# Streaming encoder trunk on one core: the last output's transposes one tile later, later splits and sums in the FFNs, one PSUM pool for two FFNs, first weights by halves of k

## The chip, the cores and the metric

The kernel runs on one core of one Trainium2 chip. The core has five engines with a queue of instructions each: PE (matrix products and transposes), DVE (VectorE), ACT (ScalarE), POOL (GpSimd) and SP (SyncE), whose queue here issues the DMAs. The metric is the device time of one execution in microseconds (us), lower is better. All names with an L and a number are lines of the kernel's file before the change; lines of the changed file are said to be so.

## The reference

One inference step of a hybrid encoder of two layers, for 512 new frames of one stream (with no history) and 16 frames each of 8 running streams, 640 tokens in all, with D_MODEL = 1024 and D_FF = 2816, all in float32:

```python
def swiglu(x, w_gate, w_up, w_down):
    return (jax.nn.silu(x @ w_gate) * (x @ w_up)) @ w_down
...
    for l in range(DEPTH):
        x = x + 0.5 * swiglu(rmsnorm(x, norm_g[l, 0]), ffn_w_gate[l, 0], ffn_w_up[l, 0], ffn_w_down[l, 0])
        hn = rmsnorm(x, norm_g[l, 1])
        if l % 2 == 0:
            out, ab_state = mixer_ab(hn, ab_state, ab_w_in, ab_w_out, ...)
        else:
            out, c_state = mixer_c(hn, c_state, gdn_w_in, gdn_w_out, ...)
        x = x + out
        x = x + 0.5 * swiglu(rmsnorm(x, norm_g[l, 2]), ffn_w_gate[l, 1], ffn_w_up[l, 1], ffn_w_down[l, 1])
    return rmsnorm(x, norm_f), ab_state, c_state
```

mixer_ab is an mLSTM beside a Mamba-2 SSD, mixer_c a gated DeltaNet. The change touches neither of them: it touches the four FFNs (the SwiGLU blocks), the start, and the last output with the last RMSNorm.

## The kernel before, in words

**Tiles.** x lives in SBUF for the whole run, transposed: eight tiles x[0] to x[7] of 128 features by 640 tokens. Two halves of 320 tokens (HT) go through PE as two matmuls, each into a PSUM bank of its own (`small`, 8 banks in an FFN).

**Products in float32.** PE takes every fp32 operand as a high and a low part (type fp32r) and makes three passes, high by high, high by low, low by high. A weight of 128x512 is *split*: ACT copies the high part (L614; L207 in the mixers and the last output), POOL subtracts it from the source for the low part (L615, L208). The parts go to a pool `wsp` of eight tiles, that is four splits. For the activations, x times the norm's gain, ACT makes the high part and DVE the low part; the factor 1/rms is multiplied in after the product.

**Stages.** Six, one after the other: FFN, mLSTM with SSD, FFN, FFN, gated DeltaNet, FFN. Each opens its own pool of PSUM banks (eight in an FFN, another layout in a mixer), so the first banks of a stage wait for the last use of those before.

**An FFN.** `first_jobs` works the first pair of column tiles (256 columns of gate and up) by plain products: four jobs `loop(0)` to `loop(3)` run over two tiles of x each, for the gate (four banks) and the first half of up (two banks), then `second(0)` and `second(1)` for the other half of up (two banks). Each split of these covers 128x512 of a weight. After `loop(3)` PE makes the sums of squares into the factors 1/rms, which DVE finishes (`rstd_cols`, from L363). Beside the loops, `loop_end(m)` makes for one pair of x tiles the block sums T that the other pairs of columns need: ACT scales both tiles (L329), DVE makes four sums (L331 to L334), ACT and DVE make high and low parts of three (L319, L320). After `loop(3)`, `loop_end` also copies the four gate banks to SBUF on ACT (L526). The silu of the first pair (L551) and its hidden product come in pieces later (`rest`).

The ten other pairs of columns go by seven products of half blocks each (a Strassen-like scheme). DVE makes the sums of weights S for it (L408, L409, L412, L415); PE makes seven block products of 12 matmul pairs (L425); DVE combines the banks. A pair ends with `hidden`: DVE multiplies gate and up (L481), ACT makes the high part of h (L483), DVE the low part (L486). Between two pairs, a job of `down_jobs` for each of four tiles of x multiplies the h of the *group before* by the down weights (L492, into two banks) and DVE adds half of each bank to x (L577). Groups are of one pair first, then two pairs.

**What sets the order.** `pipe` writes the jobs out in order: for each job its matmuls (`run`), then the sums of weights that are soon due, then its `post` (what follows on ACT and DVE), then as many splits as the freed `wsp` tiles allow, and last the load of the next weights into the raw tile whose last split this was. The instructions of each engine are chained in that order:

```python
                job.run()
                to = ready(n)
                sums(to + SUMS)
                if job.post is not None:
                    job.post()
                split(to)
            if job.then is not None:
                job.then()
```

An instruction that waits so holds everything behind it on its engine. What stands outside `pipe` (the mixers, the start, the last output) is ordered by a scheduler.

**The start.** `load_x` issues the loads on SP's queue: x in four chunks of 256 features (`xg4` to `xg7`), the gains, and the first 256 columns of gate and up in halves of 128 columns (all of k, 1024). PE transposes x (L283), DVE or ACT copies it from PSUM (L286), ACT makes the high parts of x times the gain (L307), DVE the low parts (L308), then squares and their sum for the norm (L296, L299, L300).

**The last output.** `finish` takes the last group of down products (four tiles of h) and the last RMSNorm, for three token tiles (384 columns) and then for two (256). For each of the eight tiles of x: 12 matmuls into a bank (L2081), DVE adds it to x (L2083), ACT squares x (L2088; L2086 for the first tile) and scales it by the gain (L2091), DVE adds the square to the sum (L2089), PE transposes the scaled tile (L2095), and DVE and ACT copy the rows out by turns (L2098). `output` makes the factors from the sum, multiplies the rows and stores them.

## Time and profile before

| | us |
|---|---|
| median of three runs | 3036.93 |
| lowest and highest | 3025.48, 3037.0 |
| the profiled execution's own time | 3035.38 |
| its span (first to last instruction) | 3033.7 |
| PE busy in the span | 2901.8 |
| DVE busy | 1884.2 |
| POOL busy | 1474.1 |
| ACT busy | 1255.1 |

The mean clock granted to PE is 0.977 of full speed. In the rows that the prediction quotes, a list of waits gives the instruction that waits, the one waited for, and then the sum in us, how often, and the longest. A row of windows gives the window, its length, the busy time and count of PE, PE's weight loads, DVE, ACT and POOL, the granted clock, the busy share of the DMA engines and GB/s. A row of the timeline gives the start, the length, the engine and the line, and in brackets how long the engine had waited and for what. Names ahead of an arrow are what is written, behind it what is read.

### The profile page before, as it was taken

How to read it: one execution, taken by the hardware profiler on the slowest of the kernel's cores; microseconds unless marked ns; L12 is line 12 of the kernel's file. 1: busy time of each engine (PE TensorE's matmuls, PEld its weight loads, DVE VectorE, ACT ScalarE, POOL GpSimd, SP SyncE). 2: the span in 40 equal slices, each digit the busy share in tenths (PEclk: the TensorE clock that was granted, in tenths of full speed). 3: DMA queues.
4: the chain of work that ended last, by engine and by line, in shares of the span. 5: the costliest groups of instructions: out<-in, count | busy, mean ns of one | idle time of the engine just before them, and what ended most of it. 6: DMA issues, size and time to landing. Idle time of an engine off the chain costs nothing. (4 is left out here: it accounts for less than half of the span.)

```text
span 3033.7 us, 51436 instructions
## 1 busy us (share of the span) xinstructions
PE 2901.8 (96%) x19910; PEld 2784.1 (92%) x19910; DVE 1884.2 (62%) x3547; ACT 1255.1 (41%) x2655; POOL 1474.1 (49%) x1039
## 2 busy tenths in 40 slices
PE   7999999999999999999998999999999999999995
PEld 7999998988989889999998999999888898899994
DVE  7666655233566677666656666657777656766654
ACT  5333334333344344333344333335555455333334
POOL 3766662322223126677635766734222223676672
PEclk9999999999999999999999999999999999999999
DMA  3222222222223222222222222221221312222222
GB/s 102 88 76 82 84 84 58 86 86 86 83 59 89 69 80 67 92 78 82 84 72 63 94 84 79 75 67 49 63 67 46 87 51 88 77 84 76 79 64 82
DMA packets 245160, 232.14 MB, mean 77 GB/s; under 512 B 22135, under 2 KB 221956, under 8 KB 244918
## 3 DMA queue, kind: packets, MB, share of 16 engines
q1 hardware_dynamic: 244918, 228.87, 24.6%
q8 instruction: 158, 2.59, 0.4%
q14 instruction: 84, 0.69, 0.1%
HBM read 210.23 MB, written 18.60 MB: 75 GB/s over the span
## 5 line engine op out<-in xcount | busy, mean ns | idle before, releaser
L615 POOL TENSOR_TENSOR wsp<-wraw,wsp 128x512 fp32r<-128x512 f32 x600 | 887.0, 1489 | 608.2 <-ACT wsp L614 561.3
L208 POOL TENSOR_TENSOR wsp<-wraw,wsp 128x512 fp32r<-128x512 f32 x216 | 291.4, 1357 | 848.1 <-ACT wsp L207 511.1
L425 PE MATMUL small<-xg,wsp 128*128 128x320 f32 x3840 | 593.3, 312 | 20.3 <-ACT wsp L614 8.5
L492 PE MATMUL small<-h,wsp 128*128 128x320 f32 x4032 | 597.9, 309 | 0.0
L425 PEld LDWEIGHTS small<-xg,wsp 128*128 128x128 f32 x3840 | 575.0, 190 | 24.2 <-ACT wsp L614 19.5
L492 PEld LDWEIGHTS small<-h,wsp 128*128 128x128 f32 x4032 | 593.1, 188 | 0.0
L614 ACT ACTIVATE wsp<-wraw 128x512 fp32r<-128x512 f32 x600 | 364.4, 626 | 361.5 <-PE small L425 218.5
L225 PE MATMUL big<-xg,wsp 128*128 128x320 f32 x2112 | 370.2, 323 | 0.0
L225 PEld LDWEIGHTS big<-xg,wsp 128*128 128x128 f32 x2112 | 323.2, 194 | 21.8 <-issue 20.7
L615 POOL TENSOR_TENSOR wsp<-S,wsp 128x512 fp32r<-128x512 f32 x160 | 253.6, 1597 | 47.0 <-ACT wsp L614 36.0
L425 PE MATMUL small<-extA,wsp 128*128 128x320 f32 x1440 | 253.9, 312 | 1.0 <-POOL wsp L615 0.9
L767 PE MATMUL big<-wsp,xg 128*128 128x256 f32 x1920 | 244.1, 284 | 1.5 <-DVE zs L2061 1.4
L452 DVE TENSOR_TENSOR up<-small,up 128x320 f32<-128x320 f32 x200 | 97.7, 488 | 225.9 <-PE small L425 225.9
L767 PEld LDWEIGHTS big<-wsp,xg 128*128 128x128 f32 x1920 | 233.0, 188 | 4.2 <-DVE zs L2061 2.1
L207 ACT ACTIVATE wsp<-wraw 128x512 fp32r<-128x512 f32 x216 | 136.2, 633 | 227.9 <-PE big L225 101.7
L425 PEld LDWEIGHTS small<-extA,wsp 128*128 128x128 f32 x1440 | 224.2, 190 | 2.0 <-POOL wsp L615 2.0
L425 PE MATMUL small<-extB,wsp 128*128 128x320 f32 x960 | 180.3, 310 | 0.0
L452 DVE TENSOR_TENSOR gate<-small,gate 128x320 f32<-128x320 f32 x200 | 97.7, 489 | 129.0 <-PE small L425 128.0
L577 DVE SCALAR_TENSOR_TENSOR x<-small,x 128x320 f32<-128x320 f32 x368 | 157.7, 479 | 29.9 <-PE small L492 29.1
L483 ACT ACTIVATE h<-up 128x1280 fp32r<-128x1280 f32 x40 | 51.0, 1275 | 266.1 <-DVE up L481 266.1
L425 PEld LDWEIGHTS small<-extB,wsp 128*128 128x128 f32 x960 | 151.5, 189 | 0.0
L614 ACT ACTIVATE wsp<-S 128x512 fp32r<-128x512 f32 x160 | 99.1, 627 | 110.7 <-PE small L425 60.5
(469 smaller groups left out, 4070.3 us busy)
## 6 DMA issues: line engine op xcount, KB each, us to landing
wraw<-in_ffn_w_up SPq DMA_DIRECT2D x43, 1024.0 KB
wraw<-in_ffn_w_gate SPq DMA_DIRECT2D x43, 1024.0 KB
wraw<-in_ffn_w_down SPq DMA_DIRECT2D x38, 1024.0 KB
wraw<-in_ab_w_in SPq DMA_DIRECT2D x16, 1024.0 KB
wraw<-in_gdn_w_in SPq DMA_DIRECT2D x16, 1024.0 KB
wraw<-in_ffn_w_down SPq DMA_DIRECT2D x16, 512.0 KB
wraw<-in_ab_w_out SPq DMA_DIRECT2D x32, 256.0 KB
wraw<-in_ab_w_in SPq DMA_DIRECT2D x12, 512.0 KB
```

The source lines that it names most:

```text
L207: nc.scalar.activation(out=hi, in_=src[:, i : i + n], func=AF.Copy)
L208: nc.gpsimd.tensor_tensor(lo, src[:, i : i + n], hi.bitcast(F32), ALU.subtract)
L225: self.nc.tensor.matmul(ps[:, half, :HT], lhsT=wp, rhs=ap[:, half * HT : half * HT + HT], start=(k == 0 and i == 0), stop=(k == n - 1 and ...
L425: self.nc.tensor.matmul(ps, lhsT=unit.parts[wp][:, k], rhs=acts[k][:, ap], start=(first and k == 0 and i == 0), stop=(last and k == ND // ...
L452: nc.vector.tensor_tensor(c(dst), bank[b], c(src), ALU.add)
L483: nc.scalar.activation(out=hi, in_=u, func=AF.Copy)
L492: self.nc.tensor.matmul(out[half], lhsT=wp, rhs=ap[:, half * HT : half * HT + HT], start=(first and i == 0), stop=(last and i == 2))
L577: nc.vector.scalar_tensor_tensor(x[:, i], out[i], 0.5, x[:, i], ALU.mult, ALU.add)
L614: nc.scalar.activation(out=u.parts[0], in_=src, func=AF.Copy)
L615: nc.gpsimd.tensor_tensor(u.parts[1], src, u.parts[0].bitcast(F32), ALU.subtract)
L767: self.nc.tensor.matmul(ps[:, t % 2, :256], lhsT=ap[:, t * P : (t + 1) * P], rhs=wp, start=(k == 0 and i == 0), stop=(k == ND - 1 and i == 2))
```

## The change

It has five parts.

1. **The last output** (`finish`): what follows the matmuls of a tile is now chained in the order written. DVE adds to x, ACT scales the tile (into `extA`, a tile of another pool), then the transposes and row copies of the *previous* tile are issued, and behind them the square and its sum. The last tile's transposes follow at the end of the group of tokens.
2. **The later h split**: for the down products that use the first pair's h (the loop's `g` is 1), DVE's low part of the pair that was just finished is made after the fourth down job, not the first. The later groups are as before.
3. **T of the last pair**: the copies of the gate banks and the block sums of the last pair of x tiles come after `second(0)`, one job later than before.
4. **One PSUM pool** serves FFNs that follow each other. There is one such place, the third and fourth stage.
5. **The first weights by halves of k**: the first gate and up are loaded as two pieces of 512 features by 256 columns each, in another order among the chunks of x.

```diff
--- before.py
+++ after.py
@@ -248,21 +248,23 @@
             nc.sync.dma_start(out=r[:, 4], in_=xs[:, col])
             chunks.append(r)
 
+        for n in w:
+            self.early[n] = self.t("wraw", [P, 2048], bufs=2).rearrange("p (k c) -> p k c", k=ND)
+
         def load_w(n, a):
-            if a == 0:
-                self.early[n] = self.t("wraw", [P, 2048], bufs=2).rearrange("p (k c) -> p k c", k=ND)
-            nc.sync.dma_start(out=self.early[n][:, :, a : a + P], in_=w[n][:, :, a : a + P])
+            nc.sync.dma_start(out=self.early[n][:, a : a + 4], in_=w[n][:, a : a + 4, :256])
 
 
         rows = self.t("R", [P, T], bufs=1)
         load_chunk(0)
         nc.sync.dma_start(out=rows[:48, :P], in_=io["norm_g"].rearrange("l s (d p) -> (l s d) p", p=P))
         load_w("gate", 0)
-        for c in range(1, 4):
-            load_chunk(c)
         load_w("up", 0)
-        load_w("gate", P)
-        load_w("up", P)
+        load_chunk(1)
+        load_chunk(2)
+        load_w("gate", 4)
+        load_chunk(3)
+        load_w("up", 4)
         for src, a, b in (
             (io["norm_f"].rearrange("(d p) -> d p", p=P), 0, 8),
             (io["mlstm_norm"].rearrange("h (d p) -> (h d) p", p=P), 8, 16),
@@ -520,7 +522,7 @@
 
         def loop_end(m):
             def go():
-                if m == 3:
+                if m == 4:
                     g, _ = res["g"], res["u"] = [tile("h", [P, 2 * T], bufs=8) for _ in range(2)]
                     for i, t in enumerate(ps["g"][0] + ps["g"][1]):
                         nc.scalar.copy(g[:, i * HT : i * HT + HT], t)
@@ -553,8 +555,8 @@
             yield
             yield from self.hidden(tile, res["g"], res["u"], h)
 
-        jobs = [Job([G[m], Q[m // 2]], loop(m), loop_end(m)) for m in range(4)]
-        return jobs + [Job([V[0]], second(0)), Job([V[1]], second(1), end)], rest()
+        jobs = [Job([G[m], Q[m // 2]], loop(m), loop_end(m) if m < 3 else None) for m in range(4)]
+        return jobs + [Job([V[0]], second(0), loop_end(4)), Job([V[1]], second(1), end)], rest()
 
     def down_jobs(self, raw, h, j0, nxt):
 
@@ -690,7 +692,8 @@
                     post()
 
                 u3[2].post = lambda post=u3[2].post, begin=begin: begin(post)
-                down[0].post = lambda post=down[0].post, rest=rest: rest(post)
+                at = 0 if g > 1 else 3
+                down[at].post = lambda post=down[at].post, rest=rest: rest(post)
                 if f == 2:
                     for job in g4:
                         job.post = lambda post=job.post: (post(), next(beside))
@@ -2071,31 +2074,40 @@
             tok = slice(ts[0] * P, (ts[-1] + 1) * P)
             m = len(ts) * P
             self.acc = self.tmp()[:, :m]
-            for jb in range(4):
-                raw = self.wload(w[:, :, jb * 256 : jb * 256 + 256], n, 256)
-                for j in (2 * jb, 2 * jb + 1):
-                    wj = self.split(raw[:, :, j % 2 * P : j % 2 * P + P], n, P)
-                    ps = self.small()[:, :m]
-                    for k, a in enumerate(acts):
-                        for i, (wp, ap) in enumerate(self.passes(wj[k], a)):
-                            nc.tensor.matmul(ps, lhsT=wp, rhs=ap[:, tok], start=(k == 0 and i == 0), stop=(k == n - 1 and i == 2))
+
+            def to_rows(j, xf):
+                ps = self.small()[:, :m]
+                for t in ts:
+                    c = (t - ts[0]) * P
+                    nc.tensor.transpose(ps[:, c : c + P], xf[:, c : c + P], self.ident)
+                for t in ts:
+                    c = (t - ts[0]) * P
+                    (nc.vector.tensor_copy if t % 2 else nc.scalar.copy)(yrows[t][:, j * P : j * P + P], ps[:, c : c + P])
+
+            last = None
+            for j in range(ND):
+                if j % 2 == 0:
+                    raw = self.wload(w[:, :, j * P : j * P + 256], n, 256)
+                wj = self.split(raw[:, :, j % 2 * P : j % 2 * P + P], n, P)
+                ps = self.small()[:, :m]
+                for k, a in enumerate(acts):
+                    for i, (wp, ap) in enumerate(self.passes(wj[k], a)):
+                        nc.tensor.matmul(ps, lhsT=wp, rhs=ap[:, tok], start=(k == 0 and i == 0), stop=(k == n - 1 and i == 2))
+                with self.in_order():
                     x = self.x[j][:, tok]
                     nc.vector.scalar_tensor_tensor(x, ps, 0.5, x, ALU.mult, ALU.add)
-                    xf = self.tmp()[:, :m]
+                    xf = self.ext("A")("", [P, T])[:, :m]
+                    nc.scalar.activation(out=xf, in_=x, func=AF.Copy, scale=self.gain[:, 48 + j : 49 + j])
+                    if last is not None:
+                        to_rows(*last)
+                    last = j, xf
                     if j == 0:
                         nc.scalar.activation(out=self.acc, in_=x, func=AF.Square)
                     else:
-                        nc.scalar.activation(out=xf, in_=x, func=AF.Square)
-                        nc.vector.tensor_tensor(self.acc, self.acc, xf, ALU.add)
-                        xf = self.tmp()[:, :m]
-                    nc.scalar.activation(out=xf, in_=x, func=AF.Copy, scale=self.gain[:, 48 + j : 49 + j])
-                    ps = self.small()[:, :m]
-                    for t in ts:
-                        c = (t - ts[0]) * P
-                        nc.tensor.transpose(ps[:, c : c + P], xf[:, c : c + P], self.ident)
-                    for t in ts:
-                        c = (t - ts[0]) * P
-                        (nc.vector.tensor_copy if t % 2 else nc.scalar.copy)(yrows[t][:, j * P : j * P + P], ps[:, c : c + P])
+                        sq = self.tmp()[:, :m]
+                        nc.scalar.activation(out=sq, in_=x, func=AF.Square)
+                        nc.vector.tensor_tensor(self.acc, self.acc, sq, ALU.add)
+            to_rows(*last)
             self.output(ts, yrows)
 
     def output(self, ts, yrows):
@@ -2128,10 +2140,13 @@
             self.load_x(0, 0, after(0))
             if stages[0][0] != "ffn":
                 self.setup(stages[0][0])
+        psum = ExitStack()
         for i, (kind, l, s) in enumerate(stages):
             with ExitStack() as section:
                 tile = self.section(section, kind)
-                self.banks(section, 8 if kind == "ffn" else 4)
+                if i == 0 or (kind == "ffn") != (stages[i - 1][0] == "ffn"):
+                    psum.close()
+                    self.banks(psum, 8 if kind == "ffn" else 4)
                 if kind == "ffn":
                     mid = stages[i + 1][0] if i + 1 < len(stages) else "ffn"
                     self.ffn(tile, l, 0 if s == "a" else 1, after(i + 1), mid if mid != "ffn" else None)
@@ -2142,6 +2157,7 @@
                 if i < len(stages) - 1:
                     kind, l, s = stages[i + 1]
                     self.preload(kind, l, 0 if s == "a" else 1)
+        psum.close()
 
 
 STAGES = (("ffn", 0, "a"), ("ab", 0, "m"), ("ffn", 0, "b"), ("ffn", 1, "a"), ("gdn", 1, "m"), ("ffn", 1, "b"))
```

At the place of part 3 in the second FFN (the one after the mLSTM), ACT's queue stood so before; `small` are PSUM banks, `wraw` raw weights, `S` sums of weights, `ext` and `h` the tiles of T:

```order
L614 ACTIVATE wsp_11789<-wraw_11581 128x512
L526 COPY h_11852<-small_11609 128x320
L526 COPY h_11852<-small_11610 128x320
L526 COPY h_11852<-small_11611 128x320
L526 COPY h_11852<-small_11612 128x320
L329 ACTIVATE h_11861<-x_90,gain 128x640
L329 ACTIVATE h_11861<-x_91,gain 128x640
L319 ACTIVATE extC_11859<-h_11861 128x320
L319 ACTIVATE extB_11858<-h_11861 128x320
L319 ACTIVATE extC_11860<-h_11861 128x320
L614 ACTIVATE wsp_11874<-wraw_11727 128x512
L614 ACTIVATE wsp_11878<-S_11770 128x512
```

and stands so now:

```order
L616 ACTIVATE wsp_11789<-wraw_11581 128x512
L616 ACTIVATE wsp_11852<-wraw_11727 128x512
L616 ACTIVATE wsp_11856<-S_11770 128x512
L528 COPY h_11886<-small_11609 128x320
L528 COPY h_11886<-small_11610 128x320
L528 COPY h_11886<-small_11611 128x320
L528 COPY h_11886<-small_11612 128x320
L331 ACTIVATE h_11895<-x_90,gain 128x640
L331 ACTIVATE h_11895<-x_91,gain 128x640
L321 ACTIVATE extC_11893<-h_11895 128x320
L321 ACTIVATE extB_11892<-h_11895 128x320
L321 ACTIVATE extC_11894<-h_11895 128x320
```

The two last rows of before, splits of the up weight and of a sum of weights, stood behind the nine rows of copies and T; now they stand ahead of them, as the second and third row.

At the place of part 2, in the first FFN, DVE's queue behind the product of gate and up stood so before (`small` are the banks of the down products):

```order
L481 TENSOR_TENSOR up_710<-gate_621,up_710 128x1280
L486 TENSOR_TENSOR h_884<-up_710,h_883 128x1280
L577 SCALAR_TENSOR_TENSOR x_84<-small_890,x_84 128x320
L577 SCALAR_TENSOR_TENSOR x_84<-small_891,x_84 128x320
L577 SCALAR_TENSOR_TENSOR x_85<-small_907,x_85 128x320
L577 SCALAR_TENSOR_TENSOR x_85<-small_908,x_85 128x320
L577 SCALAR_TENSOR_TENSOR x_86<-small_927,x_86 128x320
L577 SCALAR_TENSOR_TENSOR x_86<-small_928,x_86 128x320
L408 TENSOR_TENSOR S_957<-wraw_133_805 128x512
L409 TENSOR_TENSOR S_958<-S_957,wraw_133_805 128x512
L577 SCALAR_TENSOR_TENSOR x_87<-small_943,x_87 128x320
L577 SCALAR_TENSOR_TENSOR x_87<-small_944,x_87 128x320
```

and now:

```order
L483 TENSOR_TENSOR up_710<-gate_621,up_710 128x1280
L579 SCALAR_TENSOR_TENSOR x_84<-small_890,x_84 128x320
L579 SCALAR_TENSOR_TENSOR x_84<-small_891,x_84 128x320
L579 SCALAR_TENSOR_TENSOR x_85<-small_906,x_85 128x320
L579 SCALAR_TENSOR_TENSOR x_85<-small_907,x_85 128x320
L579 SCALAR_TENSOR_TENSOR x_86<-small_926,x_86 128x320
L579 SCALAR_TENSOR_TENSOR x_86<-small_927,x_86 128x320
L410 TENSOR_TENSOR S_956<-wraw_133_805 128x512
L411 TENSOR_TENSOR S_957<-S_956,wraw_133_805 128x512
L488 TENSOR_TENSOR h_884<-up_710,h_883 128x1280
L579 SCALAR_TENSOR_TENSOR x_87<-small_942,x_87 128x320
L579 SCALAR_TENSOR_TENSOR x_87<-small_943,x_87 128x320
```

The low part of h stands behind six of the eight additions to x, and behind two sums of weights.

At the place of part 1, ACT's queue in the first group of tokens stood so before, from the second tile's split of weights to the third tile's scaling:

```order
L207 ACTIVATE wsp_31260<-wraw_31228 128x512
L2088 ACTIVATE tmp_31154<-x_85 128x384
L2091 ACTIVATE tmp_31157<-x_85,gain 128x384
L2098 COPY xg_4951_31100<-small_31159 128x128
L2098 COPY xg_4953_31102<-small_31159 128x128
L207 ACTIVATE wsp_31292<-wraw_31290 128x512
L2088 ACTIVATE tmp_31186<-x_86 128x384
L2091 ACTIVATE tmp_31189<-x_86,gain 128x384
```

and now, over about the same stretch, a tile further on:

```order
L207 ACTIVATE wsp_31281<-wraw_31279 128x512
L2100 ACTIVATE extA_31175<-x_86,gain 128x384
L2085 COPY xg_4950_31096<-small_31177 128x128
L2085 COPY xg_4952_31098<-small_31177 128x128
L207 ACTIVATE wsp_31311<-wraw_31279 128x512
L2108 ACTIVATE tmp_31184<-x_86 128x384
L2100 ACTIVATE extA_31205<-x_87,gain 128x384
```

The row copies (`xg` from `small`) stand between the scaling and the square, and they are those of the tile before. PE's queue has the 12 matmuls of the next tile ahead of a tile's transposes there.

## The prediction

> **What bounds the kernel now.** I read the page's busy table first, then the list of PE's waits, then the windows with their granted clock, and last the timeline around each wait.

> ```profile
> PE 2901.8 (96%) x19910; PEld 2784.1 (92%) x19910; DVE 1884.2 (62%) x3547; ACT 1255.1 (41%) x2655; POOL 1474.1 (49%) x1039
> ...
> PE small L2095 <- ACT tmp L2091: 26.1, 16, 2.1
> PE small L425 <- ACT wsp L614: 8.5, 4, 2.6
> PE small L425 <- DVE x L577: 8.5, 6, 2.2
> ...
> PE small L919 <- DVE x L577: 4.5, 2, 2.6
> PE small L425 <- POOL wsp L615: 4.1, 6, 1.0
> ...
> PE small L492 <- DVE rstd L369: 3.2, 1, 3.2
> PE small L492 <- ACT h L329: 3.0, 1, 3.0
> ```

> PE sets the end: it is busy 2901.8 of 3033.7 us, and no matmul is added or removed. So only its 132 idle us, and the clock at which it runs, can change. The rows name the places (total, times, longest): sixteen waits of the last output (26.1), eight behind DVE's L577 (8.5 + 4.5 = 13.0), ten at the first pair products of the four FFNs (8.5 + 4.1 = 12.6), one at the second gate of the first FFN (3.2), one at the start of an FFN (3.0).

> A wait of 2 us costs more than itself. Windows (PE busy and count first, granted clock third from the end):

> ```profile
> 98.70:102.10 3.40, 3.36 (x14) 3.26 (x14) 3.30 (x6) 0.42 (x4) 2.56 (x2) 0.50 0.02 5
> 1163.60:1170.40 6.80, 5.77 (x20) 5.38 (x21) 6.70 (x8) 4.04 (x7) 5.61 (x4) 0.50 0.00 0
> 1610.80:1614.20 3.40, 3.40 (x15) 3.40 (x14) 3.40 (x4) 2.73 (x5) 2.64 (x2) 0.50 0.00 0
> 2587.00:2593.80 6.80, 5.90 (x21) 5.51 (x22) 6.70 (x8) 3.90 (x7) 5.74 (x4) 0.50 0.01 2
> 2617.70:2621.10 3.40, 3.19 (x12) 3.22 (x13) 3.30 (x8) 0.00 (x0) 3.40 (x3) 0.50 0.00 0
> 2600.40:2603.80 3.40, 3.40 (x26) 3.40 (x25) 1.63 (x3) 0.63 (x1) 3.40 (x3) 1.00 0.75 222
> ...
> 2583.60:2587.00 3.40, 1.05 (x8) 0.79 (x6) 3.40 (x8) 1.57 (x2) 0.00 (x0) 1.00 0.01 2
> ```

> The last row is the stretch just before one of the slow ones: PE busy 1.05 of 3.40 us, and then the clock is halved. At half clock 15 matmuls fit where 26 do (third and sixth row), so 1 - 15/26 = 0.42 of the busy time there is lost. The second, third and fourth row follow the waits on L614: (5.77 + 3.40 + 5.90) x 0.42 = 6.4 us. The first and fifth follow waits on L577: (3.36 + 3.19) x 0.42 = 2.8 us.

> [...]

> **The last output.** The tile's chain before, three token tiles and then two:

> ```profile
> 2990.76 0.56 DVE L2083 SCALAR_TENSOR_TENSOR x<-small,x 128x384 f32<-128x384 f32 x1 [1.51 <-PE small L2081]
> ...
> 2991.41 0.52 ACT L2088 ACTIVATE tmp<-x 128x384 f32<-128x384 f32 x1
> 2991.84 0.60 ACT L2091 ACTIVATE tmp<-x,gain 128x384 f32<-128x384 f32 x1
> 2991.97 1.05 DVE L2089 TENSOR_TENSOR tmp<-tmp,tmp 128x384 f32<-128x384 f32 x1 [0.65 <-ACT tmp L2088]
> 2992.49 0.55 PE L2095 MATMUL small<-ident,tmp 128*128 128x128 f32 x3 [1.77 <-ACT tmp L2091]
> ...
> 2993.70 0.27 ACT L2098 COPY xg<-small 128x128 f32<-128x128 f32 x1 [0.36 <-DVE xg L2098]
> ...
> 2995.18 0.56 DVE L2083 SCALAR_TENSOR_TENSOR x<-small,x 128x384 f32<-128x384 f32 x1 [1.51 <-PE small L2081]
> ...
> 3017.00 0.42 DVE L2083 SCALAR_TENSOR_TENSOR x<-small,x 128x256 f32<-128x256 f32 x1 [1.12 <-PE small L2081]
> ...
> 3017.84 0.49 ACT L2091 ACTIVATE tmp<-x,gain 128x256 f32<-128x256 f32 x1
> ...
> 3020.29 0.42 DVE L2083 SCALAR_TENSOR_TENSOR x<-small,x 128x256 f32<-128x256 f32 x1 [1.14 <-PE small L2081]
> ```

> A tile takes 4.42 us (2990.76 to 2995.18), of which PE waits 1.77; or 3.29, with 1.42 of waiting. With the transposes one tile later PE no longer waits for this tile's scaled copy. But the square now stands on ACT behind the copies of the tile before, DVE's sum waits for the square, and the next tile's addition stands behind the sum. That is a loop without PE: addition 0.56, scaled copy 0.60, the three row copies 0.27 + 0.36 + 0.27 (ACT, then DVE while ACT waits, then ACT, all from one bank), square 0.52, sum 0.56 (taken as L2083's; 1.05 stands there beside a split on POOL), and a little for the hand-offs: 3.2 us. For two token tiles 0.42 + 0.49 + 0.27 + 0.42 + 0.42 (square and sum taken as the addition's) and hand-offs: 2.2. Eight tiles each: 8 x (4.42 - 3.2) + 8 x (3.29 - 2.2) = 18.5. The first tile of each group has no loop yet (-2.3), the last one no cover, since its transposes and sum of squares follow at once (two groups, 0.8 each: -1.6), and a sum or two will lie beside a split, at 0.5 to 0.9 more (-1.6). I take **13**; bounds 8 (the splits that now stand inside the loop on ACT, 0.6 each, all delay it) and 23 (PE alone sets the pace).

> **The later h split.** At the first pair of an FFN:

> ```profile
> 1185.15 7.20 PE L492 MATMUL small<-h,wsp 128*128 128x320 f32 x48
> ...
> 1188.84 1.49 DVE L481 TENSOR_TENSOR up<-gate,up 128x1280 f32<-128x1280 f32 x1
> ...
> 1191.67 1.49 DVE L486 TENSOR_TENSOR h<-up,h 128x1280 fp32r<-128x1280 f32 x1 [1.34 <-ACT h L483]
> ...
> 1193.08 2.47 DVE L577 SCALAR_TENSOR_TENSOR x<-small,x 128x320 f32<-128x320 f32 x6
> ```

> DVE waits 1.34 for ACT, splits for 1.49, and only then adds the finished down banks into x. PE's next product needs such a bank. Behind L481 (ends 1190.33) the first L577 can now end at 1190.8, before PE is through its 48 matmuls (1192.35). So the 13.0 us go, less 0.5 where ACT's and POOL's splits become next, and the 2.8 of half clock: **15.3**. Late next is L486 itself: it stands behind L409, which waits for POOL, and the last two L577 stand behind L486. Their banks are needed by the seventh product, 6 x 12 x 0.15 = 10.8 us after the down products; DVE is there some 7 us after. Bounds 10 and 17.

> **T of the last pair behind the splits.** In the FFN after the mLSTM, and for contrast the waits at the same products of the first FFN (60 to 80 us):

> ```profile
> 1154.29 3.00 POOL L615 TENSOR_TENSOR wsp<-S,wsp 128x512 fp32r<-128x512 f32 x2
> ...
> 1157.32 1.75 DVE L409 TENSOR_TENSOR S<-S,wraw 128x512 f32<-128x512 f32 x1 [1.20 <-POOL wsp L615]
> ...
> 1162.17 1.27 ACT L551 ACTIVATE h<-h 128x1280 f32<-128x1280 f32 x1 [2.85 <-DVE h L547]
> ```
> ```profile
> PE small L425 <- POOL wsp L615: 1.9, 3, 1.0
> PE small L425 <- ACT wsp L614: 0.7, 1, 0.7
> ```

> PE waits for the up matrix's first split, which stands on ACT behind the silu L551; that waits for DVE, and DVE lost 1.20 us at L409 because POOL still held S. In the changed order two of three splits leave before the copies of the gate banks, so POOL is through S earlier. In the first FFN, where L409 does not wait, PE loses 1.9 + 0.7 = 2.6, and its clock stays full. The other three lose 12.6 - 2.6 = 10.0; at 2.6 each they save 2.2, and the 6.4 of half clock: **8.5**. The copies and T themselves hide beside the 48 matmuls of the second gate half. Bounds 0 and 13.

> **One PSUM pool** for the two FFNs in a row.

> ```profile
> 1567.16 0.88 DVE L577 SCALAR_TENSOR_TENSOR x<-small,x 128x320 f32<-128x320 f32 x2
> ...
> 1572.63 0.63 ACT L614 ACTIVATE wsp<-wraw 128x512 fp32r<-128x512 f32 x1 [1.50 <-PE small L492]
> ...
> 1578.19 1.18 ACT L614 ACTIVATE wsp<-wraw 128x512 fp32r<-128x512 f32 x2 [0.80 <-PE small L492]
> ...
> 1585.64 0.69 DVE L408 TENSOR_TENSOR S<-wraw 128x512 f32<-128x512 f32 x1 [7.65 <-DMA wraw<-in_ffn_w_gate]
> ```

> The 3.0 us end with the last L577 of the old pool (1568.04), whatever name the list gives; six banks are free before. But the gate load on which DVE waits at 1585.64 follows the split of 1578.19, and ahead of DVE's rstd it paces PE. That split can come 0.80 + 1.50 = 2.3 us earlier before ACT's own work binds. So **2.3**, and 0.7 comes back before the second gate half. Bounds 0 and 3.0.

> **First weights by halves of k.** The first row groups the T's subtractions (shortest, median and longest ns), the second is from the timeline:

> ```profile
> L331 DVE TENSOR_TENSOR h<-h x16: 477/486/1569, 22.5 to 2572.8; 128x320 f32<-128x320 f32 x16
> ```
> ```profile
> 44.86 0.69 DVE L408 TENSOR_TENSOR S<-wraw 128x512 f32<-128x512 f32 x1 [6.55 <-DMA wraw<-in_ffn_w_gate]
> ```

> The same bytes are loaded. PE starts its first FFN earlier, but what counts is DVE's L408 and the rstd behind it, on which PE waits 3.2. DVE's queue ahead shortens: the copy of the last x goes first, and POOL's first splits no longer run beside it (the longest L331, 1.57, stands there; the median is 0.49). I estimate **4**: three such stretches at 1.1, and one copy off the queue. Against it, three splits now head ACT's queue and hold the first scaled copies until both half loads are in. Bounds 0 and 8 (the 3.2 gone too).

> **Sum:** 13 + 15.3 + 8.5 + 2.3 + 4 = 43.1. The profiled execution took 3035.4 (1.6 below the median shown), so 2992.

> **Rivals.** (1) *The finish runs at PE's pace*: 26.1 less the two uncovered last tiles (3.2) saves 23, 10 more: 2982. For it: PE has the most work per tile; against it: the loop above. (2) *The clock pays nothing*, since the halved windows have another cause than these waits, or the shorter waits still halve it: 2992 + 9.2 = 3001. Against it stand the rows at 0.50. [...] (3) *The finish keeps its pace*, since ACT's splits wait for matmuls in front of the copies: 2992 + 13 = 3005. (4) *Slower*: at eight places L409 holds L486, the last L577 and their banks. It decides from 10.8 us after the down products, and to lose the 43 and 15 more each place must cost 7, so DVE would be 18 us late where I count 7. (5) *Little of it is real*: the pool does nothing, ACT's new head delays the start, and (2) and (3) both hold: 3035.4 - 43 + 9 + 13 + 6 = 3020.

> **Numbers.** Forecast 0.50, (1) 0.16, (2) 0.14, (3) 0.10, (5) with all that ends within 0.5% 0.06, slower 0.04. A measurement here tells 0.5% (15 us) from no change; (5) lies at its edge. Faster by over 0.5%: 0.91, within: 0.05, slower: 0.04. The range takes in (1) with part of the start's bound, and (2) and (3): 2974 to 3012.

> **What would show it.** L2095's waits down from 26.1 to some 10, and L2083 every 3.2 and 2.2 us; no PE wait on L577 at the first pairs; waits on L614 and L615 near 2.6 in each FFN, at full clock; the rstd wait in the first FFN near 2, and a new one below 1 in the fourth stage. Waits of 1.7 left in the finish, or 0.50 in the windows after the openings, would prove me wrong.

## The result and the profile after

| us | before | after |
|---|---|---|
| median | 3031.20 (4 runs) | 2993.07 (4 runs) |
| lowest and highest | 3025.07, 3037.0 | 2991.16, 2998.4 |
| profiled execution, its span | 3035.38, 3033.7 | 2991.16, 2989.4 |
| PE idle in the span | 131.9 | 100.0 |

The ratio is 0.9882, with a 95% interval of 0.9866 to 0.9898: 38 us faster by the medians. The forecast of 2992 (2974 to 3012) holds, but its sum of 43.1 doesn't hold term by term.

From the page of the kernel after, the busy row, and from its list of PE's waits the rows that answer to those before (lines of this kernel stand 2 or 3 further down than before; the last output's transposes are now L2082, its matmuls L2095, its addition L2098):

```profile
PE 2889.4 (97%) x19910; PEld 2777.9 (93%) x19910; DVE 1877.5 (63%) x3547; ACT 1250.4 (42%) x2655; POOL 1478.5 (49%) x1039
...
PE small L2082 <- ACT extA L2100: 9.0, 8, 2.4
...
PE small L427 <- ACT wsp L616: 6.2, 4, 2.4
...
PE small L427 <- POOL wsp L617: 4.8, 6, 1.0
...
PE small L494 <- DVE rstd L371: 2.7, 2, 1.6
...
PE small L922 <- DMA tmp<-in_gdn_conv_w: 2.0, 2, 1.6
```

The waits of the last output fell from 26.1 to 9.0. Those at the first pairs behind DVE's addition to x (8.5 and 4.5) are gone; what is left at one of the four is a wait for a DMA (2.0, and 1.7 before). The waits at the openings, behind ACT's and POOL's splits, fell only from 12.6 to 11.0. That at the first FFN's factors 1/rms went from 3.2 to 1.1, but a second one of 1.6 is new in the fourth stage.

Both kernels issue the same 19910 matmuls, up to the last output in the same order. So the start of the n-th matmul in either trace gives the lead at each place, and its growth over a stretch is what that stretch gained:

| stretch | gain in the two profiles, us | forecast |
|---|---|---|
| start, to behind the first FFN's factors | 4.1 | 4 (first weights) |
| first pairs of the four FFNs | 5.1 + 3.3 + 3.9 + 5.3 = 17.6 | 15.3 (later h split) |
| the four openings and the start of the fourth stage | -0.1 + 1.0 + 1.8 + 0.1 = 2.8 | 10.8 (T 8.5, pool 2.3) |
| last output | 13.2 | 13 |
| the two mixers | 4.6 + 2.0 = 6.5 | 0 |
| sum | 44.2 | 43.1 |

The start, the first pairs and the last output are near the forecast; the openings gave 8 less; and 6.5 stand in stages that the change doesn't touch. The larger part of that lies between the first matmuls of the first mixer and of the FFN behind it, here from the timelines before and after (1123.10 - 474.99 = 648.1 against 643.6):

```profile
474.99 2.36 PE L792 MATMUL big<-xg,wsp 128*64 128x320 f32 x8 [3.57 <-DVE v L1259]
...
1123.10 1.12 PE L492 MATMUL small<-xg,wsp 128*128 128x320 f32 x6 [1.76 <-DVE x L743]
```
```profile
465.85 1.46 PE L795 MATMUL big<-xg,wsp 128*64 128x320 f32 x5 [3.57 <-DVE v L1262]
...
1109.41 0.83 PE L494 MATMUL small<-xg,wsp 128*128 128x320 f32 x4 [1.76 <-DVE x L746]
```

### The profile page after: what moved, and what is told of

The parts are those of the page before. It is cut to its first block, busy times and chain, and to the rows that moved or that the text cites. A ratio compares the mean times of both kernels' runs of the same rounds, so it can differ in the third digit from the quotient of the medians.

```text
span 2989.4 us, 51425 instructions
## 1 busy us (share of the span) xinstructions
PE 2889.4 (97%) x19910; PEld 2777.9 (93%) x19910; DVE 1877.5 (63%) x3547; ACT 1250.4 (42%) x2655; POOL 1478.5 (49%) x1039
## 5 line engine op out<-in xcount | busy, mean ns | idle before, releaser
L617 POOL TENSOR_TENSOR wsp<-wraw,wsp 128x512 fp32r<-128x512 f32 x600 | 892.2, 1500 | 556.3 <-ACT wsp L616 546.1
L616 ACT ACTIVATE wsp<-wraw 128x512 fp32r<-128x512 f32 x600 | 364.3, 626 | 373.6 <-PE small L427 216.0
L617 POOL TENSOR_TENSOR wsp<-S,wsp 128x512 fp32r<-128x512 f32 x160 | 250.5, 1577 | 72.0 <-ACT wsp L616 45.0
L579 DVE SCALAR_TENSOR_TENSOR x<-small,x 128x320 f32<-128x320 f32 x368 | 157.9, 480 | 29.9 <-PE small L494 29.1
L485 ACT ACTIVATE h<-up 128x1280 fp32r<-128x1280 f32 x40 | 51.0, 1274 | 263.8 <-DVE up L483 263.8
L616 ACT ACTIVATE wsp<-S 128x512 fp32r<-128x512 f32 x160 | 99.3, 627 | 112.2 <-PE small L427 59.6
```

The source lines that it names most:

```text
L485: nc.scalar.activation(out=hi, in_=u, func=AF.Copy)
L579: nc.vector.scalar_tensor_tensor(x[:, i], out[i], 0.5, x[:, i], ALU.mult, ALU.add)
L616: nc.scalar.activation(out=u.parts[0], in_=src, func=AF.Copy)
L617: nc.gpsimd.tensor_tensor(u.parts[1], src, u.parts[0].bitcast(F32), ALU.subtract)
```

## The experiments

### One part undone at a time

**The last output as before**, the whole of `finish`:

```diff
-                    if last is not None:
-                        to_rows(*last)
-                    last = j, xf
...
+                    for t in ts:
+                        c = (t - ts[0]) * P
+                        nc.tensor.transpose(ps[:, c : c + P], xf[:, c : c + P], self.ident)
```

> The changed kernel with the last output as before (transposes of a tile right behind its own matmuls), the four other parts kept. Theory (the loop over DVE and ACT now sets the pace of the last output): 13.3 us longer than the changed kernel, all of it behind the last FFN's last product, the tiles again at 4.42 and 3.29 us. Rival (part of the 13.3 came from the splits and loads that arrive with the earlier FFNs, not from the order in the last output): less than 11 us. Mixers: by the theory that their 6.5 us come from where the halved clock windows fall, they are as in the changed kernel here, since nothing ahead of them moves; if they differ by more than 1 us, it is scatter of one execution.

Median 3007.81 (8 runs, 2997.80 to 3016.31), ratio to before 0.9927 (0.9910 to 0.9944): 14.7 over the changed kernel by the medians. The profiled execution is the slowest of the eight. Its last output took 79.8 us, against 71.5 in the kernel before, which has the same code there, and 58.3 in the changed one: 21.5 more, not 13.3. Windows of this kernel (PE busy first, granted clock third from the end):

```profile
2941.00:2944.40 3.40, 1.58 (x11) 1.26 (x10) 2.17 (x3) 1.82 (x5) 1.27 (x1) 0.99 0.01 2
2944.40:2947.80 3.40, 2.58 (x9) 2.06 (x7) 0.56 (x1) 1.03 (x3) 0.35 (x1) 0.50 0.46 154
...
2958.10:2961.50 3.40, 1.63 (x10) 1.30 (x10) 1.61 (x2) 1.66 (x3) 1.27 (x1) 1.00 0.02 7
2961.50:2964.90 3.40, 2.07 (x12) 1.75 (x11) 0.93 (x3) 1.80 (x5) 0.70 (x1) 1.00 0.00 0
```

and of the kernel before, in its last output:

```profile
2975.90:2979.30 3.40, 1.63 (x11) 1.31 (x9) 1.24 (x3) 1.92 (x4) 1.18 (x1) 1.00 0.00 0
2979.30:2982.70 3.40, 2.60 (x15) 2.28 (x15) 1.35 (x3) 1.27 (x4) 0.26 (x2) 1.00 0.48 154
...
3003.43:3006.84 3.41, 1.59 (x14) 1.59 (x14) 2.07 (x5) 1.76 (x5) 1.27 (x1) 1.00 0.92 372
3006.84:3010.25 3.41, 1.99 (x17) 1.72 (x15) 1.85 (x3) 1.67 (x4) 1.27 (x1) 1.00 0.23 89
```

With a wait of 1.77 in each tile, a window of 3.4 us that holds one of the waits whole leaves PE busy for some 1.6 us. Behind 1.58 in the one kernel the clock was halved for four windows, and once more later in that output; behind 1.63 and 1.59 in the other it was not. So the old order ran at an edge, where the busy time alone doesn't tell which way it goes: the same code took 71.5 or 79.8 us. The scatter of both kernels that have it fits that (14 us between lowest and highest of 13 runs of the kernel before in this comparison, 18.5 here; 7 in the four runs of the changed kernel), but doesn't show it: two kernels below that have the new order scatter by 15 and 19. The part is worth 13.2 between the profiles before and after, where the old order kept the full clock until PE was through (3025.73; 0.50 from 3027.31 on), and more where the clock falls. The mixers took 0.1 and 0.8 us less here than in the changed kernel.

**The h split back behind the first down product.**

```diff
-                at = 0 if g > 1 else 3
+                at = 0
```

> The changed kernel with DVE's low part of h back behind the first down product everywhere, the four other parts kept. Theory: at the first down products of the four FFNs PE waits for L579 again, 13 us of waiting in eight places, and with the windows of half clock behind them 17.6 us in the FFNs. Recorded forecast of this part: 15.3. Rival (the clock pays nothing): 12.5 to 13. In the mixers, by the theory of the windows' place: some change of either sign up to 5 us, since all behind the first FFN moves by about 5 us; by the rival that this part itself sped the mixers up: 6.5 us more there.

Median 3006.72 (6 runs, 3003.20 to 3010.49), 0.9935 (0.9918 to 0.9953), 13.7 over the changed kernel. At the four first pairs this profile lost 5.3 + 5.4 + 3.0 + 2.9 = 16.6 us. Its list of waits has the old rows again:

```profile
PE small L427 <- DVE x L579: 8.1, 6, 1.9
...
PE small L922 <- DVE x L579: 3.4, 2, 1.9
```

So 16.6 to 17.6. Beside the 12.5 counted for the waits, 4 to 5 are left, where I had counted 2.8 for the clock; the rival, that the clock pays nothing, falls. Between the profiles before and after, PE's idle time at these four places fell by 12.8 us and its busy time by 4.8. That all of the 4.8 is the clock isn't shown: the second FFN has 0.3 of it, and no window of half clock there in either profile. The mixers were 2.7 slower and 8.4 faster than in the changed kernel, with no instruction moved in them: not a gain that this part carries.

**T of the last pair ahead of the splits again.**

```diff
-                if m == 4:
+                if m == 3:
...
-        jobs = [Job([G[m], Q[m // 2]], loop(m), loop_end(m) if m < 3 else None) for m in range(4)]
-        return jobs + [Job([V[0]], second(0), loop_end(4)), Job([V[1]], second(1), end)], rest()
+        jobs = [Job([G[m], Q[m // 2]], loop(m), loop_end(m)) for m in range(4)]
+        return jobs + [Job([V[0]], second(0)), Job([V[1]], second(1), end)], rest()
```

> The changed kernel with the gate copies and the last pair's T ahead of the splits again, the four other parts kept. Theory (DVE's queue in front of the silu is what PE waits for at the openings, and the part only traded L411's wait for POOL, 1.2 us, against a stretch of the reciprocal roots beside POOL's splits, 3.0 to 5.1 us): 3 us longer in the FFNs at most, the waits on L616 in the second and sixth stage at 2.5 to 2.7 instead of 2.4 and 2.3. Recorded forecast: 8.5 longer, with 6.4 of them by the clock. Rival: 0, since the part does nothing.

Median 2992.74 (2 runs), 0.9883 (0.9825 to 0.9941): no difference from the changed kernel. At the four openings it lost 0.0 + 0.4 + 0.3 + 0.1 = 0.8 us; the waits on L616 are 7.0 instead of 6.2, those on L617 5.5 instead of 4.8. The forecast of 8.5 falls. The timeline in the second FFN, of this kernel and then of the changed one, shows the trade:

```profile
1136.13 0.17 DVE L357 TENSOR_TENSOR nr<-nr 128x5 f32<-128x5 f32 x1
...
1146.11 1.77 DVE L411 TENSOR_TENSOR S<-S,wraw 128x512 f32<-128x512 f32 x1 [1.19 <-POOL wsp L617]
...
1150.98 1.27 ACT L553 ACTIVATE h<-h 128x1280 f32<-128x1280 f32 x1 [2.83 <-DVE h L549]
...
1152.82 0.56 PE L427 MATMUL small<-xg,wsp 128*128 128x320 f32 x2 [2.61 <-ACT wsp L616]
```
```profile
1131.88 2.55 POOL L617 TENSOR_TENSOR wsp<-wraw,wsp 128x512 fp32r<-128x512 f32 x2 [8.96 <-ACT wsp L616]
...
1133.24 1.22 DVE L356 TENSOR_TENSOR nr<-nr 128x5 f32<-128x5 f32 x1
1134.40 1.29 POOL L617 TENSOR_TENSOR wsp<-S,wsp 128x512 fp32r<-128x512 f32 x1
1134.49 1.22 DVE L357 TENSOR_TENSOR nr<-nr 128x5 f32<-128x5 f32 x1
...
1143.21 1.60 DVE L411 TENSOR_TENSOR S<-S,wraw 128x512 f32<-128x512 f32 x1
...
1147.80 1.69 DVE L322 TENSOR_TENSOR xg<-h,xg 128x320 fp32r<-128x320 f32 x4
1147.91 1.27 ACT L553 ACTIVATE h<-h 128x1280 f32<-128x1280 f32 x1 [2.63 <-DVE h L549]
...
1149.76 0.56 PE L427 MATMUL small<-xg,wsp 128*128 128x320 f32 x2 [2.41 <-ACT wsp L616]
```

L411's wait for POOL (1.19) is gone, as forecast. But the two splits sent ahead now run on POOL beside DVE's reciprocal roots, where L356 and L357, on 128x5, take 1.22 instead of 0.17 and end as POOL's splits end (1134.46 and 1135.71 against 1134.43 and 1135.69). The two cost 2.1. The silu L553 waits nearly as long as without the part (2.63 against 2.83), and with it PE.

**A PSUM pool for each stage again.**

```diff
-                if i == 0 or (kind == "ffn") != (stages[i - 1][0] == "ffn"):
-                    psum.close()
-                    self.banks(psum, 8 if kind == "ffn" else 4)
+                self.banks(section, 8 if kind == "ffn" else 4)
```

> The changed kernel with a PSUM pool of its own for each stage again, the four other parts kept. Theory (the 3.1 us gained at the start of the fourth stage were lost again at the factors 1/rms, 1.6 us of waiting and one window of half clock): the first matmul of the fourth stage 3.0 us later, and after its first pair of columns less than 0.7 us later, either sign. Recorded forecast: 2.3 longer after the stage. Nothing ahead of the fourth stage moves.

Median 2996.71 (2 runs), 0.9896 (0.9832 to 0.9961), 3.6 over the changed kernel by the medians, with 8 between its two runs. In its profile the fourth stage's first products came 3.1 later, and behind its opening 2.5 were left. So the part is worth 2.5, near the 2.3 forecast, and the theory that it is nothing falls: what it gives back, 1.6 at the factors 1/rms and a window of half clock, is in part paid without it too, since two windows of half clock then stand in that opening for one.

**The first weights by halves of columns again**, with the loads in the order of before:

```diff
-            nc.sync.dma_start(out=self.early[n][:, a : a + 4], in_=w[n][:, a : a + 4, :256])
+            nc.sync.dma_start(out=self.early[n][:, :, a : a + P], in_=w[n][:, :, a : a + P])
```

> The changed kernel with the first weights loaded by halves of columns behind x again, the four other parts kept. Theory (DVE's queue in front of the factors 1/rms sets when PE goes on in the first FFN): PE's wait for rstd back from 1.1 to 3.2 us, the end of the first FFN's loops 4.1 us later, nothing else outside the mixers. Recorded forecast: 4 (0 to 8). Rival: 0 to 1, since the start waits for the same bytes.

Median 2995.49 (4 runs, 2984.92 to 2999.70), 0.9868 (0.9834 to 0.9901). The first FFN's wait for its factors is back at 3.3, and PE is 3.8 us later behind it. The 2.4 by the medians is within their scatter. The second FFN lost 2.1 more in this profile, but a kernel below that differs from the changed one in the last output alone lost 1.9 there, so I count neither.

Single profiles scatter at the start too. The first block product of the first FFN begins at 53.99 to 58.08 us in the twelve profiles with the new loads, at 55.9 in the mean, and at 59.57 and 59.86 in the two with the old ones. The difference is 4. The load that DVE's first sum of weights waits for, before and then after, goes out 3.8 us earlier, and the sum follows it (at 44.86 before):

```profile
39.63 0.40 SPq L181 DMA_DIRECT2D wraw<-in_ffn_w_gate  x1
```
```profile
35.83 0.40 SPq L181 DMA_DIRECT2D wraw<-in_ffn_w_gate  x1
...
41.36 0.69 DVE L410 TENSOR_TENSOR S<-wraw 128x512 f32<-128x512 f32 x1 [6.86 <-DMA wraw<-in_ffn_w_gate]
```

By the profiles the parts are 13.2 + 16.6 + 0.8 + 2.5 + 3.8 = 37 us (the 13.2 from the profiles before and after, since the run without that part lost 21.5 there); by the medians, undone one at a time, 14.7 + 13.7 - 0.3 + 3.6 + 2.4 = 34. The change as a whole has 38 by the medians. The 44 between the two profiles hold the mixers' 6.5 besides. Over the fourteen profiles of this study the two mixers, unchanged, took 1162.0 to 1174.3 us together; the kernel before has the highest. Their scatter is of the same size as what was gained there, so I count it as no gain of the change. The kernel that differs in the last output alone took 2.3 more in the first mixer than the changed one.

### What PE waits for at the openings

Theory now: DVE's queue ahead of the silu. Three kernels shorten or pass it.

**Sums of weights behind the products with 1/rms**, at the last of the first jobs:

```diff
-                sums(to + SUMS)
+                if not job.late:
+                    sums(to + SUMS)
                 if job.post is not None:
                     job.post()
+                sums(to + SUMS)
```

> The changed kernel with the next sums of weights (L410, L411) behind the first pair's products with 1/rms (L547, L549) on DVE, at that one job of each FFN. Theory (DVE's queue in front of the silu is what PE waits for at the openings): the silu starts 2.3 to 2.9 us earlier, the four waits on L616 (6.2 us together in the changed kernel) fall below 1 us together, POOL's 0.96 in each stays; with one or two windows of half clock fewer 6 to 12 us shorter. Rival (as recorded: the splits' place behind the copies on ACT is what PE waited for, and what is left has to do with POOL): the waits stay above 4 us together and the time within 2 us.

**The gate's products with 1/rms first** (the two L549 ahead of the four L547):

```diff
-            for i, t in enumerate(ps["q"] + ps["v"]):
-                nc.vector.tensor_tensor(u[:, i * HT : i * HT + HT], t, self.R[:, i % 2 * HT : i % 2 * HT + HT], ALU.mult)
             for i in range(2):
                 nc.vector.tensor_tensor(g[:, i * T : i * T + T], g[:, i * T : i * T + T], self.R, ALU.mult)
+            for i, t in enumerate(ps["q"] + ps["v"]):
+                nc.vector.tensor_tensor(u[:, i * HT : i * HT + HT], t, self.R[:, i % 2 * HT : i % 2 * HT + HT], ALU.mult)
```

> The changed kernel with the two products of the gate with 1/rms (L549) ahead of the four of up (L547) on DVE, at the first pair of each FFN. Theory (DVE's queue in front of the silu): the silu 1.7 us earlier, the waits on L616 from 0.8, 2.4, 0.7, 2.3 to 0, 0.7, 0, 0.6, so 4.9 us shorter, and up to 4 more by the clock. Rival (the splits wait for something else on ACT): no change.

Both are slower than the changed kernel by the medians: 3000.22 (5 runs, 2987.17 to 3006.13; 0.9889, 0.9861 to 0.9918) and 3008.30 (6 runs, 3006.28 to 3009.46; 0.9931, 0.9914 to 0.9947). The interval of the first overlaps that of the changed kernel; in the profiles, the four FFNs lost 11.8 and 16.4 us. From the timeline of the first of the two, in the second FFN:

```profile
1148.35 1.27 ACT L553 ACTIVATE h<-h 128x1280 f32<-128x1280 f32 x1
...
1149.53 3.86 DVE L322 TENSOR_TENSOR xg<-h,xg 128x320 fp32r<-128x320 f32 x4
...
1156.42 1.27 ACT L485 ACTIVATE h<-h 128x1280 fp32r<-128x1280 f32 x1 [5.76 <-DVE h L483]
...
1158.26 0.56 PE L427 MATMUL small<-extA,wsp 128*128 128x320 f32 x2 [3.18 <-ACT wsp L618]
```

The theory held for its own wait: the silu no longer waits, and PE gained 4.3 us there, 1.4 of it by a window of half clock that didn't come. Then the four low parts of T (L322) fell beside POOL's splits and took 3.86 instead of 1.69, the hidden product L483 came late behind them, and L485 took the silu's place as what holds the splits on ACT. PE lost 7.5 in the products behind. In the second kernel the four took 3.83. Both theory and rival had left that out.

**The silu two jobs later, the hidden product too:**

```diff
+            yield
             next(blocks)
+            yield
             nc.scalar.activation(out=res["g"], in_=res["g"], func=AF.Silu)
...
-                    for job in g4:
+                    for job in g4 + u4[:2]:
```

> The changed kernel with the pieces of the first pair that stand at the openings moved down ACT's and DVE's queues: the low parts of the last block of T one job later, the silu two jobs later, the hidden product two jobs later. Theory (at the openings the splits stand on ACT behind the silu, and the silu waits for DVE; shortening DVE's queue only let L485 take the silu's place as the holder): now nothing that waits for DVE stands ahead of the splits, so the waits on L616 (6.2 us in four places) and POOL's (4.8) fall below 2 us together, and with the windows of half clock behind them the openings are 9 to 15 us shorter. Rival (DVE beside POOL's splits is slowed so much that the adds which free banks, or the sums of weights, are late next): the waits come back under another name, within 4 us of the changed kernel or slower.

Median 2997.51 (3 runs, 2993.60 to 2997.96; 0.9895, 0.9872 to 0.9917). The rival holds: PE passes the first products without a wait, and loses more later than it gained (6.1 us net in the four FFNs), again behind L485, which waits for L483. In the second FFN:

```profile
1160.31 1.27 ACT L485 ACTIVATE h<-h 128x1280 fp32r<-128x1280 f32 x1 [4.56 <-DVE h L483]
...
1162.15 0.56 PE L427 MATMUL small<-xg,wsp 128*128 128x320 f32 x2 [2.18 <-ACT wsp L618]
```

### Two edits that beat the changed kernel

**The sum of squares one tile later**, in the last output:

```diff
                     nc.vector.scalar_tensor_tensor(x, ps, 0.5, x, ALU.mult, ALU.add)
+                    if sq is not None:
+                        nc.vector.tensor_tensor(self.acc, self.acc, sq, ALU.add)
...
                         nc.scalar.activation(out=sq, in_=x, func=AF.Square)
-                        nc.vector.tensor_tensor(self.acc, self.acc, sq, ALU.add)
+            nc.vector.tensor_tensor(self.acc, self.acc, sq, ALU.add)
```

> The changed kernel with DVE's sum of squares of a tile behind the next tile's addition to x, in the last output alone. Theory (the loop: addition, scaled copy, row copies, square, sum, next addition, 3.2 to 3.4 us in the first group of tokens): with the sum out of it PE or ACT set the pace, 2.6 to 2.9 us a tile, 3 to 5 us shorter in the first group and less than 1 in the second. Rival (the transposes wait for ACT's splits): the pace stays at 3.2 to 3.4, within 1 us.

Median 2986.07 (2 runs; 0.9858, 0.9796 to 0.9920). DVE's addition in the changed kernel's first group of tokens, and then in this one:

```profile
2946.03 0.55 DVE L2098 SCALAR_TENSOR_TENSOR x<-small,x 128x384 f32<-128x384 f32 x1
...
2949.26 0.55 DVE L2098 SCALAR_TENSOR_TENSOR x<-small,x 128x384 f32<-128x384 f32 x1
...
2952.69 0.55 DVE L2098 SCALAR_TENSOR_TENSOR x<-small,x 128x384 f32<-128x384 f32 x1
```
```profile
2944.30 0.56 DVE L2098 SCALAR_TENSOR_TENSOR x<-small,x 128x384 f32<-128x384 f32 x1 [0.73 <-PE small L2095]
...
2946.71 0.56 DVE L2098 SCALAR_TENSOR_TENSOR x<-small,x 128x384 f32<-128x384 f32 x1 [0.73 <-PE small L2095]
```

The loop of 3.23 or 3.43 us (with a split inside) becomes 2.41, and now DVE waits for PE. The last output took 49.3 us instead of 58.3: 9.0 saved where I expected 3 to 6.

**Both edits so far in one** gave 2985.88 (2 runs; 0.9873, 0.9819 to 0.9928).

> Both edits in one: the silu and the hidden product later, and the sum of squares of the last output one tile later. They touch different stages, so the gains add: by the theory 9 to 15 and 9 us (what the last output measured alone), 18 to 24 us shorter than the changed kernel; by the rival 5 to 13.

It is 7 below the changed kernel by the medians, the rival's sum. The kernel before was 3.9 faster in this comparison too, and the two profiles differ by 2.9, so it may be less.

**The hidden product of the first pair six jobs later**, behind the pair's seven splits, and the silu three:

```diff
+            yield
             next(blocks)
-            nc.scalar.activation(out=res["g"], in_=res["g"], func=AF.Silu)
-            yield
-            yield
+            for n in range(7):
+                if n == 2:
+                    nc.scalar.activation(out=res["g"], in_=res["g"], func=AF.Silu)
+                yield
...
-                    for job in g4:
+                    for job in g4 + u4 + g3[:2]:
```

> The changed kernel with the sum of squares of the last output one tile later, and at the first pair of each FFN the silu three jobs later and the hidden product of the first pair (L483, L485, L488) six jobs later, behind all seven splits of the pair. Theory (whatever stands on ACT ahead of the splits and waits for DVE becomes PE's wait; with silu later alone, L485 had become it, 4.6 us behind DVE): nothing that waits for DVE stands ahead of the splits until DVE has caught up, so the waits of the openings on L618 and L619, 11 us in the changed kernel, fall below 3 us, and with the clock 9 to 15 us are saved in the FFNs, beside 9 in the last output: 18 to 24 shorter than the changed kernel. Rival (DVE's own work at the openings is the bound, wherever the holder stands): the wait comes back behind DVE's adds or sums, the FFNs within 4 us, 5 to 13 shorter in all.

> As the run beside it, with the gate's products with 1/rms (L549) ahead of up's (L547) and the silu only two jobs later. Theory: the silu still needs DVE, but its products come 1.7 us earlier, so it holds nothing: within 2 us of the run beside it. Rival (the silu, one job earlier, holds the splits behind DVE as before): 3 to 8 us slower than the run beside it.

The first has a median of 2972.35 (4 runs, 2966.08 to 2973.29), 0.9807 (0.9789 to 0.9826) of the kernel before, and 20.7 below the changed one. The kernel before was 3.5 faster in this comparison, and the two profiles differ by 17.8, so the gain is 17 to 21, at or just under the 18 to 24 of the theory. The second, with the gate's products first, 2973.68 (4 runs, 2972.50 to 2976.41; 0.9818, 0.9798 to 0.9837): the same within the scatter, as its theory had it. The first one's page and its only row of waits on splits:

```profile
PE 2881.9 (97%) x19910; PEld 2767.6 (93%) x19910; DVE 1890.3 (64%) x3547; ACT 1249.3 (42%) x2655; POOL 1486.4 (50%) x1039
...
PE small L427 <- POOL wsp L619: 6.8, 10, 0.9
```

ACT's row is gone, and no window of half clock follows the openings of the second and sixth stage. POOL's row grew from 4.8 to 6.8 where I expected below 3: ten waits of less than a microsecond, POOL's queue being next. From the first block product of each on, the four FFNs gave 0.8 + 2.0 + 1.1 + 2.1 = 6.0 us in the profile, below the 9 to 15 expected and above the 4 of the rival.

## Why the prediction came out right, and where it was wrong

- **The last output**: right in mechanism and size (13 against 13.2). The loop without PE was put at 3.2 and 2.2; it was 3.2 to 3.4 and, once going, 1.8. Two windows of half clock between the two groups of tokens (2957.71 to 2964.54), which the sum doesn't have, cost 2.2 by its own 0.42 (of 5.3 busy), and the faster second group paid for them; so the size is in part luck. Rival (1), PE's own pace, came about only once the sum of squares left the loop (13.2 + 9.0 = 22.2 of its 23).
- **The later h split**: right, 15.3 against 16.6 to 17.6. What comes on top of the waits was put too small (2.8 against 4 to 5). The 6.8 us at half clock behind the first pair of the fourth stage (from 1641.50 before, from 1619.7 after) stand in no term, and stayed. L486, named as late next, didn't hold PE.
- **T behind the splits**: the step that failed, 8.5 (its terms 2.2 and 6.4 add to 8.6) against 0.8. That "two of three splits leave before the copies of the gate banks, so POOL is through S earlier" is what happened, and L409's wait went, but it bought next to nothing, since the same splits then stretched DVE's work in front of the silu. That silu ran on DVE's time was in the row quoted there (2.85 behind L547); I took only L409's 1.20 out of that queue and put nothing in. The 6.4 for the clock failed with it. Windows of the changed kernel behind its openings:

```profile
66.60:70.00 3.40, 3.40 (x14) 3.10 (x13) 3.40 (x4) 3.15 (x5) 2.64 (x3) 0.50 0.00 0
1152.10:1155.50 3.40, 3.40 (x15) 3.40 (x14) 3.40 (x4) 2.90 (x5) 2.64 (x2) 0.50 0.00 0
1571.90:1575.30 3.40, 3.40 (x15) 3.40 (x14) 3.30 (x6) 2.89 (x7) 2.98 (x3) 0.50 0.46 160
2561.80:2568.60 6.80, 5.89 (x22) 5.89 (x23) 6.63 (x6) 3.15 (x5) 6.04 (x4) 0.50 0.01 2
```

  They are 17.0 us in all, as many as before (6.8 + 3.4 + 6.8). The first stands in the first FFN, which had none there; the third follows the wait for the factors 1/rms in the fourth stage, which has none behind its splits now.
- **One PSUM pool**: 2.3 against 2.5, right in size in part by luck. The new wait at the fourth stage's factors was foreseen below 1 and was 1.6, with a window of half clock behind it; that windows of half clock would go elsewhere in that stage stands in no term.
- **First weights**: right, 4 against 3.8 to 4.1, and by the queue it named: of the subtractions in front of the second load, the two that took 1.57 and 1.58 beside POOL before take 0.48 now. One profile alone, with a scatter of 4 us, would not have shown it.
- **The base.** The sum was taken from the profiled execution, 3035.4, which was 4 above the median of all runs of the kernel before (3031.2). So that the time was met within 1 us is luck: the saving was put 5 too high (8 too much at the openings, less 2 too little at the first pairs), and the base 4 too high.
- **Rival (2)**, that the clock pays nothing, is wrong for the first pairs (16.6 to 17.6 us where the waits have 12.5) and right in effect for the openings. Rivals (3), (4) and (5) fell.

## What to carry to other kernels

Before an operation is moved ahead on one queue, write down what will run beside it on the others, and price those again: here POOL's splits, sent earlier, cost DVE more than they saved (2.1 us against 1.2). When PE waits for an engine that is itself waiting, look for everything on that queue which waits for the slow engine: moving the first holder only promoted the next, and the gain came when all of them stood behind the work that PE needs. A loop between two engines is broken by taking one link a turn later. And a sum of savings is set against the median of the runs, since the one profiled execution can lie some microseconds off it.

## What the runs showed of the hardware

**DVE beside POOL.** A DVE operation of 128x5 (L356, L357 of the changed kernel) took 1.22 us while POOL worked on a split of 1.3, and 0.17 otherwise; four of 128x320 (L322) took 3.86 instead of 1.69. L353, also on 128x5, took 1.18 to 1.20 beside a split, and 0.17 in the first mixer with no split beside it. What makes DVE slower there no run shows. For the operations of 128x5 the price was not their own length but what was left of POOL's split: L356 and L357 ended within 0.03 us of one.
